# A two-block transformer kernel: first modulation columns on column quarters with zero products between, a third buffer for the modulation weights, and background steps tied to data

## The chip, the cores and the metric

The kernel runs on one core of a Trainium2 chip. TensorE (PE in the rows; PEld are its weight loads) does the matrix products, VectorE is DVE, ScalarE is ACT, GpSimd is POOL and SyncE is SP; POOL and SP here issue transfers almost alone. The metric is the device time of one launch in microseconds (us); less is better.

## The reference, cut to what matters

A first block of two layers (token mixer, then a gated convolutional feed-forward) runs on 256 latent and 256 context tokens of width 1024, then a second block (mLSTM and attention, then a product-key expert layer) on the result. Every normalised input is scaled and shifted by vectors that come from a conditioning vector alone:

```python
def adaln_params(cvec, w_ada, b_ada):
    m = jax.nn.silu(cvec) @ w_ada + b_ada        # 1024 -> 6144
    return jnp.split(m, 6, axis=-1)              # shift, scale, gate, shift, scale, gate
...
    h = modulate(rmsnorm(x, g1), sh1, sc1)       # the same with hc for the context
    z = h @ w_in
    ...
    x = x + gt1 * (mix @ w_out)
    x = x + gt2 * conv_ffn(modulate(rmsnorm(x, g2), sh2, sc2), w_up, ffn_conv, w_down)
```

There are three such weight matrices `w_ada` (two layers of the first block, one of the second), 25 MB each, used for one or two conditioning vectors (`c` for the latent tokens, `x` in the kernel's names for the context).

## The kernel before

All products run in fp32-like precision from two fp32r halves: `weight` loads a 128x1024 weight into `wraw` (three buffers, SP's queue), ACT rounds it to `whi` (L259), DVE makes the rest `wlo` (L262), and `gemm` does three products per tile (L278): hi·hi, hi·lo, lo·hi. A product with 512 columns is one matmul; 24 of them use up one weight of the first layer's feed-forward.

**The modulation vectors** are made in two ways. The first two sections of layer 0 (shift and scale of the first norm) are needed at once, and `first_norm` makes them on TensorE: four chunks of 512 outputs (`columns(0..3)`, scale and shift of the first 512 features, then of the last 512), whose weights `adan` (two transfers of 1 MB a chunk) are the moving operand while the silu of the two conditioning vectors (`cc_s`) is stationary, two columns wide. Chunks 0 and 1 are plain fp32 products (L421; each fp32 product is two matmuls in the trace), chunks 2 and 3 are split by ACT and DVE into `adah` and `adal` and done as fp32r products (L418, L419). ACT copies the sums to `adar` (L423), four small products (`po`, L426) turn the row into columns, DVE adds the bias (L432, L434). Meanwhile ACT squares `x` and `xc`, DVE adds them (`nacc`), TensorE sums over partitions (L479), DVE takes the inverse root from `nv` on (L481), and TensorE spreads it over partitions (`pt`, L494). Then `modulated` makes `nw` (L508, DVE), `h_hi` (L509, ACT) and `h_lo` (L510, DVE), and `tokens_gemm` multiplies them by `win_tm` (L666): 96 matmuls for `v` and `va`, then 96 for queries and keys (`pqk`), whose results pass DVE (`e`, L715) to transposes on TensorE (L721).

All other sections are made by `ada_chunk` in the background: POOL's queue loads 128 outputs x 1024 weights into `adaw` (512 KB, two buffers), and DVE multiplies by the silu vector `cvec` and sums along the row (`junk`, L365), one step for each conditioning vector. `background` gives these steps low priorities; the list scheduler places them in DVE's order between the layer's own work, once and for all at build time. Each engine then takes its instructions in that order. `later0` hands them out: 24 chunks of layer 0 in three lots (FIRST0 = 14, up to EARLY0 = 17, the rest), and in layer 0's feed-forward (`where == 3`) 66 two-vector or one-vector chunks of layers 0, 1 and 2, 122 DVE steps in all: 48 steps of two-vector chunks, 32 one-vector chunks of layer 1 (each with a transfer of its own), then 32 and 10 steps for the second block. Ahead of the last 42 come the second block's silu vectors (`load_cvec`): a transfer into an `adaw` buffer, a tanh on ACT (L354) into another, and a DVE step (L356).

The feed-forward (`ffn`) runs `up(0)`, `up(1)`, `down(0)`, `up(2)`, `down(1)`, `down(2)`: 68 weights in layer 0.

Of the kernel before, what the change touches and what calls it, by code (L numbers as in the profile page):

```python
# [11 lines left out]
F32 = mybir.dt.float32  # L12
F32R = mybir.dt.float32r
# [9 lines left out]
P = 128  # L23
D = 1024
# [11 lines left out]
RSQRT_MAGIC = 0x5F3759DF  # L36
NE = 128
# [38 lines left out]
def first_constants():  # L76
    k = Pack()
    k.add("ident", np.eye(P))
    k.add("ones", np.ones((P, P)))
    k.add("pairs", np.tile(np.eye(2), (2, 1)))  # L80
# [130 lines left out]
class Kernel:  # L211
# [137 lines left out]


    def load_cvec(self, idx, raw, th):

        self.nc.gpsimd.dma_start(raw, self.d["cvec"][idx].partition_broadcast(P))
        self.nc.scalar.activation(th, raw, AF.Tanh, scale=0.5)  # L354
# [29 lines left out]
    def first_norm(self, pool, tokens, hi, lo):  # L384
# [3 lines left out]
        cc = self.prm["ccol"]  # L388
        th = self.t(pool, [P, 2 * KT], F32, "cc_th", 1)
        nc.scalar.activation(th, cc, AF.Tanh, scale=0.5)  # L390
        s = self.t(pool, [P, KT, 2], F32, "cc_s", 1)
        nc.vector.scalar_tensor_tensor(s.rearrange("p a b -> p (a b)"), th, 1.0, cc, op0=OP.add, op1=OP.mult)
        s4 = self.t(pool, [P, KT, 4], F32R, "cc_s4", 1)
        self.split(s4[:, :, 0:2], s4[:, :, 2:4], s)
# [10 lines left out]
        def columns(ch):  # L405
            half, scale = ch // 2, ch % 2 == 0
            p = self.acc()
            n = 4 if half else 2
            for kp in range(KT // 2):
                raw = w[ch, kp // 2][:, kp % 2 * 2:kp % 2 * 2 + 2, :]  # L410
                if half:
                    wh = self.t(pool, [P, 2, 512], F32R, "adah", 2)
                    wl = self.t(pool, [P, 2, 512], F32R, "adal", 2)
                    self.split(wh, wl, raw)
                for kk in range(2):
                    kt = kp * 2 + kk
                    if half:
                        nc.tensor.matmul(p[0:4, :], s4[:, kt, :], wh[:, kk, :], start=kt == 0, stop=False)  # L418
                        nc.tensor.matmul(p[0:4, :], s4[:, kt, :], wl[:, kk, :], start=False, stop=kt == KT - 1)  # L419
                    else:  # L420
                        nc.tensor.matmul(p[0:2, :], s[:, kt, :], raw[:, kk, :], start=kt == 0, stop=kt == KT - 1)  # L421
            row = self.t(pool, [4, 512], F32, "adar", 2)
            nc.scalar.mul(row[0:n, :], p[0:n, :], 0.5)  # L423
            q = self.po()
            for j in range(4):
                nc.tensor.matmul(q[:, j * 2:j * 2 + 2], row[0:n, j * P:j * P + P], self.k["pairs"][0:n, :], start=True, stop=True)  # L426
# [10 lines left out]
        for kt in range(KT):  # L437
            self.squares(kt, ((self.x, TOK, None), (self.xc, TOK, None)))
# [11 lines left out]
        return ps  # L450

# [97 lines left out]
    def trunk_layer(self, l, cv, later):  # L549
# [9 lines left out]
        with ExitStack() as st:  # L559
# [45 lines left out]
            with ExitStack() as st2:  # L605
                fp = st2.enter_context(tc.tile_pool(name=f"ffn{l}", bufs=1, reuse_waits="tile"))
                first = None if full else self.first_up(l, fp)
                later(3)
# [75 lines left out]
    def mixer_d(self, l, mp, hi, lo, mix, lam, pva, fill, begin, later):  # L684
# [986 lines left out]
def build(ctx, tc, d, out, tap=None, stop=None):  # L1671
# [12 lines left out]
    def later0(where):  # L1684
        if where == 0:
            both.extend(zip(("l0c", "l0x"), k.vecs))
            third.extend([j for s in (2, 3, 4) for j in k.ada_jobs(ap, 0, s, both, "n2g0" if s == 4 else None)])
            k.background(third[:FIRST0], 55)
# [4 lines left out]
        if where == 3:  # L1693
            b1 = [("l1" + n[2], v) for n, v in both]
            jobs = k.ada_jobs(ap, 0, 5, both)
            jobs += [j for s in (1, 0) for j in k.ada_jobs(ap, 1, s, b1, "n1g1" if s == 1 else None)]
            jobs += [j for s in (2, 3, 4, 5) for j in k.ada_jobs(ap, 1, s, b1[:1], "n2g1" if s == 4 else None)]
            k.background(jobs, FSTEP)
            c2 = [k.load_cvec(j, *[k.t(ap, [P, D], F32, "adaw", 2) for _ in range(2)]) for j in (2, 3)]
            second.extend([("l2c", c2[0]), ("l2x", c2[1])])  # L1700
            more = [j for s in (1, 0) for j in k.ada_jobs(ap, 2, s, second, "nmix" if s == 1 else None)]
            rest.extend([j for s in (2, 3, 4, 5) for j in k.ada_jobs(ap, 2, s, second[:1], "nffn" if s == 4 else None)])
            k.background(more + rest[:EARLY2], FSTEP, FSTEP * len(jobs))
# [33 lines left out]
```

## Time and profile before

| | |
|---|---|
| median of 3 runs | 2045.8 us (2042.17 to 2057.86) |
| profiled execution | 2045.38 us, of which the span is 2043.6 us |
| busy share of the span | PE 97%, PEld 88%, DVE 82%, ACT 48%, POOL 3% |
| mean granted clock of TensorE | 0.989 of full speed |

A busy TensorE counts matmuls whose ends are modelled, so the number of matmuls in a stretch tells more than its busy share. Stretches that the text speaks of: the start (0 to 95 us), layer 0's feed-forward (about 270 to 640 us).

### The profile page before, as it was taken

Reading aid. Unit: us, or ns where it says so; the run is one execution under the profiler, and the core shown is the slowest. Engines: PE = TensorE matmul, PEld = TensorE weight load, DVE = VectorE, ACT = ScalarE, POOL = GpSimd, SP = SyncE. Lnnn points to the kernel's source line nnn. Section 1 sums busy time; section 2 is a strip of 40 time slices with the busy share of each in tenths; the row PEclk is TensorE's granted clock in tenths of the full one; section 3 lists DMA queues with packets and bytes.
Section 4 is the critical chain, followed back from the end, with each engine's and each line's share of the span. In section 5 each row is a group of like instructions: output and inputs, shape, how many; then the busy total and the mean of one; then the engine's idle time right before and its main releaser. Section 6 shows DMA issues by size and latency. Waiting matters only on the chain. (4 is left out here: it accounts for less than half of the span.)

```text
span 2043.6 us, 38424 instructions
## 1 busy us (share of the span) xinstructions
PE 1979.9 (97%) x15072; PEld 1804.8 (88%) x15072; DVE 1673.9 (82%) x3488; ACT 985.5 (48%) x1682; POOL 71.1 (3%) x138
## 2 busy tenths in 40 slices
PE   7999999998999999999999999999999999999999
PEld 3777778886888889999788888999999999999999
DVE  5898889876987689987767679988988898898775
ACT  5476343321324766545345654546544444444444
POOL 0100001111110000000000000000000000000000
PEclk9999999999999999999999999999999999999999
DMA  7631446776673346775243253454455555555554
GB/s 289 209 131 63 134 150 210 228 229 224 207 223 110 120 135 223 265 273 178 73 134 104 83 179 126 159 189 157 155 194 179 181 190 185 178 186 186 182 190 156
DMA packets 98965, 355.97 MB, mean 174 GB/s; under 512 B 11296, under 2 KB 12192, under 8 KB 97248
## 3 DMA queue, kind: packets, MB, share of 16 engines
q1 hardware_dynamic: 77616, 279.21, 41.3%
q0 software_dynamic: 19232, 70.72, 10.8%
q10 hardware_dynamic: 1936, 3.59, 0.5%
q8 instruction: 118, 1.93, 0.4%
q14 instruction: 63, 0.52, 0.1%
HBM read 352.42 MB, written 1.05 MB: 173 GB/s over the span
## 5 line engine op out<-in xcount | busy, mean ns | idle before, releaser
L259 ACT CAST whi<-wraw 128x1024 fp32r<-128x1024 f32 (+2 forms) x524 | 537.9, 1028 | 399.5 <-PE pH L278 100.2
L262 DVE TENSOR_TENSOR wlo<-wraw,whi 128x1024 fp32r<-128x1024 f32 (+3 forms) x552 | 628.2, 1141 | 102.4 <-ACT whi L259 100.7
L1549 PE MATMUL out<-w_hi,whi 128*128 128x256 f32 x1024 | 284.6, 278 | 0.2 <-ACT w_hi L268 0.2
L1549 PE MATMUL out<-w_hi,wlo 128*128 128x256 f32 x1024 | 283.1, 277 | 0.0
L1549 PE MATMUL out<-w_lo,whi 128*128 128x256 f32 x1024 | 282.8, 277 | 0.0
L365 DVE SCALAR_TENSOR_TENSOR junk<-adaw,cvec 128x1024 bf16<-128x1024 f32 x192 | 234.6, 1222 | 54.2 <-DMA adaw<-ada_in 52.6
L1549 PEld LDWEIGHTS out<-w_hi,whi 128*128 128x128 f32 x1024 | 192.4, 188 | 0.3 <-ACT w_hi L268 0.3
L1549 PEld LDWEIGHTS out<-w_hi,wlo 128*128 128x128 f32 x1024 | 192.4, 188 | 0.1
L1549 PEld LDWEIGHTS out<-w_lo,whi 128*128 128x128 f32 x1024 | 192.1, 188 | 0.1
L278 PE MATMUL acc<-h_hi,whi 128*128 128x256 f32 (+1 forms) x880 | 169.7, 330 | 11.0 <-DVE xc L642 4.9
L268 ACT CAST w_hi<-act 128x256 fp32r<-128x256 f32 x128 | 51.9, 406 | 236.7 <-PE out L1549 228.3
L278 PE MATMUL pH<-p_hi,whi 128*128 128x256 f32 x1128 | 160.5, 283 | 2.2 <-ACT act L1480 2.2
L278 PE MATMUL acc<-h_lo,whi 128*128 128x256 f32 (+1 forms) x880 | 161.0, 322 | 0.1
L278 PE MATMUL acc<-h_hi,wlo 128*128 128x256 f32 (+1 forms) x880 | 158.6, 320 | 0.5 <-DVE wlo L262 0.4
L278 PEld LDWEIGHTS acc<-h_hi,whi 128*128 128x128 f32 x880 | 131.9, 192 | 27.4 <-ACT h_hi L268 5.1
L278 PE MATMUL pH<-p_lo,whi 128*128 128x256 f32 x1128 | 153.9, 279 | 0.0
L278 PE MATMUL pH<-p_hi,wlo 128*128 128x256 f32 x1128 | 153.8, 279 | 0.0
L278 PEld LDWEIGHTS acc<-h_hi,wlo 128*128 128x128 f32 x880 | 131.2, 189 | 14.1 <-DVE wlo L262 1.2
L278 PEld LDWEIGHTS pH<-p_hi,whi 128*128 128x128 f32 x1128 | 141.1, 189 | 2.6 <-ACT act L1480 2.4
L278 PEld LDWEIGHTS acc<-h_lo,whi 128*128 128x128 f32 x880 | 131.8, 191 | 12.7 <-issue 0.3
L278 PEld LDWEIGHTS pH<-p_hi,wlo 128*128 128x128 f32 x1128 | 140.8, 189 | 0.0
L278 PEld LDWEIGHTS pH<-p_lo,whi 128*128 128x128 f32 x1128 | 140.6, 189 | 0.0
(572 smaller groups left out, 3293.2 us busy)
## 6 DMA issues: line engine op xcount, KB each, us to landing
adaw<-ada_in POOLq DMA_DIRECT2D x128, 512.0 KB, 4.5
wraw<-pu_in SPq DMA_DIRECT2D x128, 512.0 KB, 3.3
wraw<-pv_in SPq DMA_DIRECT2D x128, 512.0 KB, 3.4
wraw<-wup_in SPq DMA_DIRECT2D x88, 512.0 KB, 4.5
wraw<-win_fm_in SPq DMA_DIRECT2D x44, 512.0 KB, 3.7
wraw<-wdn_in SPq DMA_DIRECT2D x32, 512.0 KB, 4.5
wraw<-wout_in SPq DMA_DIRECT2D x24, 512.0 KB, 4.0
adan<-ada0n_in SPq DMA_DIRECT2D x8, 1024.0 KB, 15.0
```

Source lines behind the costliest of these rows:

```text
L259: nc.scalar.copy(hi[:, :n], raw[:, :n])
L262: nc.vector.tensor_sub(lo[:, s], raw[:, s], hi[:, s].bitcast(F32))
L268: self.nc.scalar.copy(hi, src)
L278: nc.tensor.matmul(ps, a[:, k, :], b[:, k, :], start=first and j == 0, stop=last and j == len(todo) - 1)
L365: nc.vector.scalar_tensor_tensor(junk, w, 0.5, cv, op0=OP.mult, op1=OP.mult, accum_out=self.ada[key][:, nt:nt + 1])
L1549: nc.tensor.matmul(part(m), x[:, m, :], y, start=False, stop=False)
```

## The change

Three things change in the code, and the scheduler's order with them. (1) `columns` treats all four chunks alike: plain fp32 products, the stationary operand widened from 2 to 32 columns by zeros, and the eight 128-row slices put on four 32-column quarters of the array in turn (`tile_position=(0, r)`), whose four partial sums the `pairs` products add. The splits `adah`/`adal` go. Between them `idle` puts products of a zero tile `z` (bf16, 128x512), 32 and 8 around the halves of chunk 0, one for each of the eight squares, and 4, 3, 3 after chunks 0 to 2; those after a chunk depend on its `adar` row through a DVE step that writes zeros made from it. (2) In layer 0's feed-forward the chunks use the pool `fp` with three `adaw` buffers in place of two, the second block's conditioning vectors are loaded ahead into `ap`'s two buffers, and the tanh goes into an `fp` buffer. (3) The constant 0.5 in the chunk step becomes a one-column tile `half`, made by `after` from a result that has to exist first: the last `v` copy for the first lot, and the last `h_lo` for the feed-forward's.

```diff
+    def after(self, x):
+        self.half = self.sm([P, 1], "half", bufs=1)
+        self.nc.vector.tensor_scalar(self.half.bitcast(I32), x.bitcast(I32), 0, HALF_BITS, op0=OP.bitwise_and, op1=OP.bitwise_or)
...
-        w = self.t(pool, [P, D], F32, "adaw", 2)
+        w = self.t(pool, [P, D], F32, "adaw", 2 if pool is self.ap else 3)
         nc.gpsimd.dma_start(w, self.d[f"ada{l}"][nt - 16 if l == 0 else nt])
         for key, cv in vecs:
-            junk = self.t(pool, [P, D], BF16, "junk", 1)
-            nc.vector.scalar_tensor_tensor(junk, w, 0.5, cv, op0=OP.mult, op1=OP.mult, accum_out=self.ada[key][:, nt:nt + 1])
+            junk = self.t(self.ap, [P, D], BF16, "junk", 1)
+            nc.vector.scalar_tensor_tensor(junk, w, self.half, cv, op0=OP.mult, op1=OP.mult, accum_out=self.ada[key][:, nt:nt + 1])
...
-            for kp in range(KT // 2):
-                raw = w[ch, kp // 2][:, kp % 2 * 2:kp % 2 * 2 + 2, :]
-                if half:
-                    wh = self.t(pool, [P, 2, 512], F32R, "adah", 2)
-                    wl = self.t(pool, [P, 2, 512], F32R, "adal", 2)
-                    self.split(wh, wl, raw)
...
-                        nc.tensor.matmul(p[0:2, :], s[:, kt, :], raw[:, kk, :], start=kt == 0, stop=kt == KT - 1)
-            row = self.t(pool, [4, 512], F32, "adar", 2)
-            nc.scalar.mul(row[0:n, :], p[0:n, :], 0.5)
+            for kt in range(KT):
+                r = kt % 4 * 32
+                if ch == 0 and kt % 4 == 0:
+                    self.idle(z, (32, 8)[kt // 4])
+                nc.tensor.matmul(p[r:r + 32, :], s[:, kt, :], w[ch, kt // 4][:, kt % 4, :], start=kt < 4, stop=kt >= 4, tile_position=(0, r))
+            row = self.t(pool, [P, 512], F32, "adar", 2)
+            nc.scalar.mul(row, p, 0.5)
+            if ch < 3:
+                self.idle(z, (4, 3, 3)[ch], row[:, 0:1])
...
         columns(0)
         for kt in range(KT):
+            self.idle(z, 1)
             self.squares(kt, ((self.x, TOK, None), (self.xc, TOK, None)))
...
+    def idle(self, z, n, x=None):
+        if x is not None:
+            self.nc.vector.tensor_scalar(z[:, 0:2].bitcast(I32), x.bitcast(I32), 0, 0, op0=OP.bitwise_and, op1=OP.bitwise_or)
+        p = self.att()
+        for _ in range(n):
+            self.nc.tensor.matmul(p, z[:, 0:P], z, start=True, stop=True)
...
+        if full:
+            self.after(v[:, 3, 0:1])
+            later("v")
...
         if where == 3:
+            k.after(k.h[1][:, KT - 1, 2 * TOK - 1:2 * TOK])
             b1 = [("l1" + n[2], v) for n, v in both]
-            jobs = k.ada_jobs(ap, 0, 5, both)
...
+            raws = []
+            for j in (2, 3):
+                raw = k.t(ap, [P, D], F32, "adaw", 2)
+                nc.gpsimd.dma_start(raw, k.d["cvec"][j].partition_broadcast(P))
+                raws.append(raw)
+            jobs = k.ada_jobs(fp, 0, 5, both)
...
-            c2 = [k.load_cvec(j, *[k.t(ap, [P, D], F32, "adaw", 2) for _ in range(2)]) for j in (2, 3)]
+            def vectors():
+                for j in (2, 3):
+                    second.append((("l2c", "l2x")[j - 2], k.silu2(j, raws[j - 2], k.t(fp, [P, D], F32, "adaw", 3))))
+            k.background([vectors], 0, FSTEP * len(jobs))
```

In TensorE's order at the start, the first `tokens_gemm` products (L666, in the changed file L680) stood ahead of most of chunk 2's products (L418, L419). Before:

```order
L494 MATMUL pt_208<-nacc_35_153,consts_73 128x128 x4
L421 MATMUL acc_217<-adan_109,cc_s_98 2x512
L421 MATMUL acc_217<-adan_111,cc_s_98 2x512 x4
L426 MATMUL po_228<-consts_73,adar_226 128x2 x4
L418 MATMUL acc_263<-adah_264,cc_s_17_100 4x512
L666 MATMUL att_359<-whi_114,h_hi_90 128x512
L666 MATMUL att_360<-whi_114,h_hi_90 128x512
L666 MATMUL att_361<-whi_114,h_hi_90 128x512
L666 MATMUL att_362<-whi_114,h_hi_90 128x512
```

After, at the same place (L423 are the quarter products, L430 the small ones that turn a row, L463 the zero products):

```order
L423 MATMUL acc_332<-adan_125,cc_s_100 32x512 x4
L423 MATMUL acc_332<-adan_127,cc_s_100 32x512 x4
L430 MATMUL po_348<-consts_73,adar_341 128x2 x4
L463 LDWEIGHTS idle_96
L463 MATMUL att_344<-idle_96 128x512
...
L680 MATMUL att_385<-whi_114,h_hi_90 128x512 x2
L680 MATMUL att_385<-whi_114,h_lo_91 128x512
L423 MATMUL acc_357<-adan_129,cc_s_100 32x512 x4
L680 MATMUL att_385<-whi_114,h_lo_91 128x512
```

The first token product now stands behind the whole of chunk 2, with its row and three zero products. A little ahead of this, twelve zero products stand between the fifth and the sixth of the eight products that sum the squares (L492):

```order
L430 MATMUL po_192<-consts_73,adar_184 128x2 x4
L492 MATMUL acc_247<-consts_73,nacc_39_203 128x1
...
L463 LDWEIGHTS idle_96
L463 MATMUL att_187<-idle_96 128x512
...
L463 MATMUL att_242<-idle_96 128x512
L492 MATMUL acc_247<-consts_73,nw_244 128x1
```

Before, the eight stood together, ahead of chunk 0's small products.

ACT's order after, at the start: chunk 2's row `adar_341` stands behind all eight `h_hi` of the first half, of which these are the last.

```order
L522 ACTIVATE h_hi_90<-nw_318,ada_l0x_78 128x256
L522 ACTIVATE h_hi_90<-nw_325,ada_l0c_77 128x256
L522 ACTIVATE h_hi_90<-nw_325,ada_l0x_78 128x256
L425 ACTIVATE adar_341<-acc_332 128x512
L363 ACTIVATE adan_375<-adan_375 128x1024
```

So the first token product waits for DVE's work on the whole first half, through this row.

DVE's order in the feed-forward, the last one-vector chunks. Before, two chunk steps (L365) stand to a weight (L262):

```order
L262 TENSOR_TENSOR wlo_4292<-wraw_4290,whi_4291 128x1024
L365 SCALAR_TENSOR_TENSOR junk_2750,ada_l1c_79<-adaw_2748,cvec_78_352 128x1024
L365 SCALAR_TENSOR_TENSOR junk_2754,ada_l1c_79<-adaw_2752,cvec_78_352 128x1024
L642 SCALAR_TENSOR_TENSOR x_67<-acc_4223,ada_l0c_77,x_67 128x256
L642 SCALAR_TENSOR_TENSOR xc_89<-acc_4223,ada_l0x_78,xc_89 128x256
L262 TENSOR_TENSOR wlo_4325<-wraw_4323,whi_4324 128x1024
```

After (L374 is the chunk step, L263 the weight's, L365 the silu step of the second block's vectors, whose transfers now stand some fifty chunks earlier on POOL's queue):

```order
L263 TENSOR_TENSOR wlo_4322<-wraw_4320,whi_4321 128x1024
L374 SCALAR_TENSOR_TENSOR junk_2800,ada_l1c_79<-adaw_2798,half_2520,cvec_75_378 128x1024
L374 SCALAR_TENSOR_TENSOR junk_2804,ada_l1c_79<-adaw_2802,half_2520,cvec_75_378 128x1024
L656 SCALAR_TENSOR_TENSOR x_67<-acc_4253,ada_l0c_77,x_67 128x256
L656 SCALAR_TENSOR_TENSOR xc_89<-acc_4253,ada_l0x_78,xc_89 128x256
L263 TENSOR_TENSOR wlo_4355<-wraw_4353,whi_4354 128x1024
L374 SCALAR_TENSOR_TENSOR junk_2808,ada_l1c_79<-adaw_2806,half_2520,cvec_75_378 128x1024
L365 SCALAR_TENSOR_TENSOR cvec_711_2817<-adaw_2815,adaw_2524 128x1024
L365 SCALAR_TENSOR_TENSOR cvec_709_2813<-adaw_2811,adaw_2522 128x1024
```

The two silu steps stand together now and wait for no transfer issued just before. Over all, the 32 one-vector chunks are spread over 16 weights before and over 13 after. On POOL's and DVE's queues no chunk stands behind another wait than that for its own buffer, before and after.

## Rows read from the trace of the kernel before

**Rows 1.** Busy time by stretch: matmuls in brackets, then PEclk, DMA share, GB/s.

```profile
33.00:38.00 5.00, 4.53 (x13) 2.99 (x13) 5.00 (x11) 4.99 (x10) 0.00 (x0) 0.66 1.02 406
...
470.00:480.00 10.00, 9.56 (x42) 7.55 (x41) 6.85 (x11) 2.11 (x2) 1.11 (x3) 1.00 0.78 240
480.00:490.00 10.00, 6.29 (x27) 4.56 (x26) 7.03 (x12) 0.00 (x0) 2.11 (x4) 1.00 0.75 254
490.00:500.00 10.00, 8.34 (x36) 6.50 (x35) 4.97 (x8) 1.99 (x2) 0.53 (x1) 1.00 0.53 149
500.00:510.00 10.00, 7.88 (x28) 6.00 (x27) 4.52 (x7) 3.52 (x4) 1.05 (x2) 0.83 0.65 211
510.00:520.00 10.00, 10.00 (x45) 8.11 (x44) 9.93 (x15) 4.68 (x6) 1.05 (x2) 1.00 0.57 185
```

**Rows 2.** Timeline, 490 to 502 us: start, length, engine; in brackets the idle time before.

```profile
494.85 1.06 ACT L354 ACTIVATE adaw<-adaw 128x1024 f32<-128x1024 f32 x1 [17.68 <-DMA adaw<-cvec_in]
...
497.46 0.53 POOL L353 DMA_DIRECT2D adaw<-cvec_in  x1 [8.13 <-DVE cvec L356]
```

**Rows 3.** DVE's waits from 420 to 560 us: total, times, longest.

```profile
DVE junk L365 <- DMA adaw<-ada_in: 24.1, 20, 2.9
```

**Rows 4.** Timeline of the start.

```profile
17.69 0.40 ACT L463 ACTIVATE nw<-xc 128x256 f32<-128x256 f32 x1
...
19.58 0.38 PE L479 MATMUL acc<-consts,nacc 128*128 128x1 f32 x2
19.68 0.59 ACT L423 ACTIVATE adar<-acc 2x512 f32<-2x512 f32 x1 [1.59 <-PE acc L421]
...
21.56 0.16 DVE L481 TENSOR_SCALAR nv<-acc 128x4 f32<-128x4 f32 x1 [2.63 <-PE acc L479]
...
25.51 1.16 PE L494 MATMUL pt<-nacc,consts 128*128 128x128 f32 x8
...
26.60 4.45 PE L421 MATMUL acc<-adan,cc_s 128*2 128x512 f32 x10
...
26.71 0.48 DVE L508 SCALAR_TENSOR_TENSOR nw<-x,ada_l0c,pt 128x256 f32<-128x256 f32 x1 [0.96 <-PE pt L494]
27.11 0.47 DVE L508 SCALAR_TENSOR_TENSOR nw<-xc,ada_l0x,pt 128x256 f32<-128x256 f32 x1
...
28.28 1.22 DVE L262 TENSOR_TENSOR wlo<-wraw,whi 128x1024 fp32r<-128x1024 f32 x1
...
31.73 1.05 PE L426 MATMUL po<-consts,adar 2*128 2x2 f32 x8 [0.68 <-ACT adar L423]
...
33.02 0.51 ACT L509 ACTIVATE h_hi<-nw,ada_l0c 128x256 fp32r<-128x256 f32 x1 [0.40 <-DVE ada_l0c L432]
...
33.58 1.25 PE L666 MATMUL att<-whi,h_hi 128*128 128x512 f32 x4 [0.47 <-ACT h_hi L509]
```

**Rows 5.** TensorE's timeline where queries and keys end.

```profile
84.42 0.63 PE L666 MATMUL acc<-whi,h_lo 128*128 128x512 f32 x2
...
89.04 0.62 PE L666 MATMUL po<-wlo,h_hi 128*128 128x512 f32 x2
92.47 1.82 PE L721 MATMUL att<-consts,e 128*128 128x128 f32 x8 [2.82 <-DVE e L715]
93.94 3.06 PE L278 MATMUL acc<-h_hi,whi 128*128 128x512 f32 x8
```

**Rows 6.** The same timeline where attention's value products stand on two column halves.

```profile
122.14 1.09 PE L799 MATMUL po<-aT,vtm 128*64 128x128 f32 x14
```

**Rows 7.** DVE groups by shape: busy us, mean ns; L780 reads a one-column scalar.

```profile
L269 DVE TENSOR_TENSOR g_lo<-f_s,g_hi 128x512 fp32r<-128x512 f32 x22 | 15.1, 686 | 0.0
...
L780 DVE SCALAR_TENSOR_TENSOR e<-e,rsm,e 128x512 f32<-128x512 f32 x16 | 12.0, 747 | 2.1 <-ACT e L779 2.1
```

**Rows 8.** Transfers of 420 to 500 us (KB, median us to landing); then all of `adaw`.

```profile
adaw<-ada_in POOLq DMA_DIRECT2D x21, 512.0 KB, 4.6
...
DMA to landing us min/median/max: 3.6/4.5/7.9
```

More of the change, by code (lines that the diff above doesn't have):

```diff
@@ L36 @@
 RSQRT_MAGIC = 0x5F3759DF
+HALF_BITS = 0x3F000000
 NE = 128
@@ L388, in first_norm @@
         cc = self.prm["ccol"]
+        z = self.t(pool, [P, 512], BF16, "idle", 1)
+        nc.vector.memset(z, 0.0)
         th = self.t(pool, [P, 2 * KT], F32, "cc_th", 1)
         nc.scalar.activation(th, cc, AF.Tanh, scale=0.5)
[L391 to L394, printed above, removed]
+        s = self.t(pool, [P, KT, 32], F32, "cc_s", 1)
+        nc.gpsimd.memset(s, 0.0)
+        nc.vector.scalar_tensor_tensor(s[:, :, 0:2], th.rearrange("p (a b) -> p a b", b=2), 1.0, cc.rearrange("p (a b) -> p a b", b=2), op0=OP.add, op1=OP.mult)
         w = {}
@@ L407, in columns @@
             p = self.acc()
-            n = 4 if half else 2
-            for kp in range(KT // 2):
-                raw = w[ch, kp // 2][:, kp % 2 * 2:kp % 2 * 2 + 2, :]
-                if half:
-                    wh = self.t(pool, [P, 2, 512], F32R, "adah", 2)
-                    wl = self.t(pool, [P, 2, 512], F32R, "adal", 2)
-                    self.split(wh, wl, raw)
[L415 to L420, printed above, removed]
-                        nc.tensor.matmul(p[0:2, :], s[:, kt, :], raw[:, kk, :], start=kt == 0, stop=kt == KT - 1)
-            row = self.t(pool, [4, 512], F32, "adar", 2)
-            nc.scalar.mul(row[0:n, :], p[0:n, :], 0.5)
+            for kt in range(KT):
[7 more added lines that the diff above has]
+                self.idle(z, (4, 3, 3)[ch], row[:, 0:1])
             q = self.po()
             for j in range(4):
-                nc.tensor.matmul(q[:, j * 2:j * 2 + 2], row[0:n, j * P:j * P + P], self.k["pairs"][0:n, :], start=True, stop=True)
+                nc.tensor.matmul(q[:, j * 2:j * 2 + 2], row[:, j * P:j * P + P], self.k["pairs"], start=True, stop=True)
             qv = q[:, 0:8].rearrange("p (j v) -> p v j", v=2)
@@ L1687, in later0 @@
             third.extend([j for s in (2, 3, 4) for j in k.ada_jobs(ap, 0, s, both, "n2g0" if s == 4 else None)])
+        if where == "v":
             k.background(third[:FIRST0], 55)
@@ L1693, in later0 @@
         if where == 3:
+            k.after(k.h[1][:, KT - 1, 2 * TOK - 1:2 * TOK])
             b1 = [("l1" + n[2], v) for n, v in both]
-            jobs = k.ada_jobs(ap, 0, 5, both)
-            jobs += [j for s in (1, 0) for j in k.ada_jobs(ap, 1, s, b1, "n1g1" if s == 1 else None)]
-            jobs += [j for s in (2, 3, 4, 5) for j in k.ada_jobs(ap, 1, s, b1[:1], "n2g1" if s == 4 else None)]
-            k.background(jobs, FSTEP)
-            c2 = [k.load_cvec(j, *[k.t(ap, [P, D], F32, "adaw", 2) for _ in range(2)]) for j in (2, 3)]
-            second.extend([("l2c", c2[0]), ("l2x", c2[1])])
-            more = [j for s in (1, 0) for j in k.ada_jobs(ap, 2, s, second, "nmix" if s == 1 else None)]
+            fp = k.fp
+            raws = []
[4 more added lines that the diff above has]
+            jobs = k.ada_jobs(fp, 0, 5, both)
+            jobs += [j for s in (1, 0) for j in k.ada_jobs(fp, 1, s, b1, "n1g1" if s == 1 else None)]
+            jobs += [j for s in (2, 3, 4, 5) for j in k.ada_jobs(fp, 1, s, b1[:1], "n2g1" if s == 4 else None)]
+            k.background(jobs, FSTEP)
+            def vectors():
+                for j in (2, 3):
+                    second.append((("l2c", "l2x")[j - 2], k.silu2(j, raws[j - 2], k.t(fp, [P, D], F32, "adaw", 3))))
+            k.background([vectors], 0, FSTEP * len(jobs))
+            more = [j for s in (1, 0) for j in k.ada_jobs(fp, 2, s, second, "nmix" if s == 1 else None)]
+            early = [j for s in (2, 3) for j in k.ada_jobs(fp, 2, s, second[:1])]
             rest.extend([j for s in (2, 3, 4, 5) for j in k.ada_jobs(ap, 2, s, second[:1], "nffn" if s == 4 else None)])
-            k.background(more + rest[:EARLY2], FSTEP, FSTEP * len(jobs))
+            k.background(more + early[:EARLY2], FSTEP, FSTEP * len(jobs))
     k.trunk_layer(0, None, later0)
```

5 lines of the change are left out of this document (4 added, 1 removed).

## The prediction

> **What bounds the kernel now.** TensorE is busy for 97% of the span, so only stretches in which it does fewer matmuls than its full rate can give anything back. I read first the busy time by stretch, counting matmuls; then, where they are missing, the timeline and the waits of the engine that TensorE waited for; then the order before and after at those places. The change touches two: the start (to about 95 us) and layer 0's feed-forward.
>
> In the feed-forward 10 us hold 45 products of 512 columns at full rate, .222 us each. From 470 to 510 us they hold 42, 27, 36 and 28: 133 in place of 180 [rows 1]. The missing 47 are 10.4 us, and no other stretch of the feed-forward lacks as many. The cause is on ACT: its tanh (L354) stood idle 17.68 us for the second block's conditioning vector [rows 2], with every later rounding of a weight behind it in ACT's order; the second vector's transfer waited 8.13 us on POOL for a buffer. Both queue behind the chunk steps, which are late themselves: DVE waited 24.1 us for their weights between 420 and 560 us [rows 3]. The arithmetic fits. A buffer's turn is landing 4.6 [rows 8], issue .53 [rows 2] and the DVE step, 1.22 by a step of the same size [rows 4]: 6.35, with two buffers 3.18 us per one-vector chunk. A weight lasts TensorE 24 x .222 = 5.33 us, and 32 such chunks lie over 16 weights, 2.67 us each. Each chunk is .51 late, the 32 together 16 us, more than the two weights that three buffers hold ahead (10.7 us).
>
> At the start TensorE makes its first token product at 33.58 and ends queries and keys at 89.04 + .46 = 89.5 [rows 4, 5], with chunk 2's and 3's columns between. At 33 to 38 us the granted clock is .66 (partly at 1.2, partly at 2.4 GHz) after a stretch with little but a row of small products [rows 1, 4]. After 89.5 it waits 2.82 us for DVE's `e`, behind chunk steps, and the next eight products take 3.06 us [rows 5].
>
> **The change part by part: the feed-forward.** The conditioning vectors are loaded before its first chunks are used up, so the tanh waits for no transfer of its own. If nothing else is late there, all 10.4 us come back; this cannot be more, since TensorE is otherwise at rate. What is late next? The chunk steps. The scalar `half` is read from memory, and a DVE step with such a scalar takes .747 us against .686 without [rows 7], .061 more; 122 steps in the feed-forward make 7.4 us of DVE time, covered by the 24.1 us of waits that three buffers take away. A turn is now 4.6 + .53 + 1.28 = 6.41, over three buffers 2.14 us. But the scheduler has spread the 32 one-vector chunks over 13 weights, not 16: 13 x 5.33 / 32 = 2.17 us each. So the third buffer is used up almost to the last by the denser order: it is just in time, without reserve except the two weights held ahead. I take back 1.0 us of the 10.4 (between 0 and the 32 x .061 = 2.0 that the scalar costs where it is tight): **-9.4 us**.
>
> **The start.** Chunk 0's row needs ACT, whose last square ends at 18.1; with the copy .59 and the small products 1.05 [rows 4] that is 19.7. The sums of squares took from 19.58 to `nv` at 21.56, 2.0 us, and now come after, with twelve zero products in their midst. No row has a zero product; as one matmul of 512 columns it is bounded by .231 us (twenty token products from 84.42 to 89.04 [rows 5]) and twice that at 1.2 GHz: 2.8 to 5.5 us. `nv` comes at 24.5 to 27.2, not 21.56. From `nv` to the first `nw` are 5.15 us [rows 4]: 29.7 to 32.4. DVE then has eight `nw` and five `h_lo`, .40 us apart (26.71 to 27.11), and two weight steps of 1.22, 7.6 us, before the eighth `h_hi`; with that (.51), chunk 2's row behind it on ACT (.59), its small products (1.05) and three zero products (.7 to 1.4) the first token product stands at 40.2 to 43.6 us, seven to ten later than before.
>
> In return the path from there is shorter. Before, it took 55.9 us. Now it has 192 products of .231 (44.4), chunk 3 and one set of small products (1.05). A chunk without quarters costs sixteen matmuls of .43 (ten from 26.60 in 4.45 us [rows 4]), 6.9 us. Two column halves already work side by side here: fourteen matmuls of 128 columns in 1.09 us, .078 each, against 1.16 / 8 = .145 for L494's of the same length on the whole array [rows 4, 6]. I take a quarter, 1.7 us, with 3.4 and 6.9 as ends. That gives 47.2 us, up to 2.0 more if the clock is at .66 again for 5 us: the end of queries and keys at 87.4 to 92.8, in the middle .6 later than the 89.5 of before. The removed ACT and DVE splits (eight each) were beside TensorE's work and give nothing of their own.
>
> The Trainium skill ("TensorE: Matmul & The Clock Gate", Part 3) reports 2.38 times for three column tiles, less than one for one. By that figure chunk 3 would cost about 2.9 us, and the end would come 1.2 later; the two halves in this trace show nearly a full factor of two, and no row has three or four.
>
> Behind it the wait for `e` can go (2.82 us) and with it the slow products (eight at .231 are 1.85, not 3.06): 4.0 us. The first chunk step now waits for the last `v` copy, half of the 192 products on, at about 66 to 70 us, two transfers having landed before; of 28 steps eleven, not thirteen, stand ahead of `e`. The two left over, 2.6 us, and the scalar's .061 on all 28 (1.7 us) are done later, in a stretch in which DVE is nearly as full as TensorE. I keep -1.6 of the -4.0. Together the start gives **-1.0 us**, between -6.1 and +3.3.
>
> The steps that the second `half` holds back were not ahead of the last `h_lo` before either, so that part is costed at nothing; its cover is the order itself. Later layers only get the scalar: 22 steps x .061, 1.3 us of DVE time beside TensorE's work.
>
> **Sum.** -9.4 - 1.0 = -10.4 us. Against the profiled execution, 2045.38 us of which 1.8 lie around the span, that is 2035.0; the median of the runs shown is .4 higher. **Predicted: 2035 us**, .5% less.
>
> **The rivals.** *The good ends meet.* The zero products run and keep the clock at 2.4 GHz, the end of queries and keys is 87.4, the whole 4.0 us behind it come back, and the feed-forward gives all 10.4: -6.1 - 10.4 = -16.5, 2029 us. Against it speaks that between the halves of chunk 0 and the sums there is little for TensorE but small products, after which the clock fell at 33 us. Some of what DVE postpones would also have to vanish for more than 1%.
>
> *The quarters do not work side by side*, so the change does not do what it says. Chunk 0's second half would pass ACT's squares by 1.4 us, chunk 1's by 2.6, chunk 3 costs 5.2 more: 9.2, and 2044 us. The halves speak against it [rows 6], though they are not quarters.
>
> *The third buffer is outrun, and the kernel is slower.* Place: the 13 weights with the 32 one-vector chunks, 45 transfers of .524 MB in 69 us, 340 GB/s, where before 48 took 85 us. At 470 to 490 us a DMA share of .78 and .75 goes with 240 and 254 GB/s [rows 1], which puts the limit at 308 to 339: the demand stands at it. DVE's order is fixed, so a late chunk holds back the `wlo` behind it and so TensorE. If landing goes to the longest seen, 7.9 us [rows 8], a chunk takes 3.24 us, 1.07 late, the 32 together 34; less the 10.7 held ahead 23.5 us of stall, which eats the 10.4 and leaves +12: 2057 us. The kernel is slower than before from a landing of about 6.8 us on. Against it: at 308 GB/s the 45 transfers take 76.6 us, 7.3 too many, still within the 10.7.
>
> The Trainium skill ("Trainium Kernel Development and Optimization", Key Constraints) says that transfers from SP, ACT and POOL run on the same 16 engines and interleave. By that rule the third buffer buys nothing beyond the engines' limit and this rival's mechanism holds; the landing of 4.6 at a share of .75 to .78 does not yet show it.
>
> **How the numbers follow.** The forecast's own case, 2031 to 2040, has a chance of .55. The good ends (2024 to 2031) have .17, of which .09 are below 2025, the quarters without effect or a start at its bad end (2040 to 2048) .16, the outrun buffer (over 2048) .12, of which .05 are above 2066. The range 2024 to 2048 leaves out about .15. The runs of before lie .8% apart, so 1% (20 us) is about what a measurement can tell from no change: faster by over 1% .09, slower by over 1% .05, within 1% .86.
>
> **What would show it.** In the profile after: no long wait of ACT at the tanh, about 45 matmuls in every 10 us of the feed-forward, DVE's waits for `adaw` in it well below 24 us, a landing below 6 us; the first token product near 42 us, queries and keys ending near 90, and a short wait for `e` or none. I am wrong if the first token product comes by 36 us, if TensorE lacks products where the one-vector chunks are, or if the stretch from 95 to 270 us changes by more than 5 us, for which I have no term.

## The result, and the profile after

The changed kernel is slower: median 2073.22 us (four runs, 2072.33 to 2076.91) against 2050.36 us of the kernel before (four runs, 2042.17 to 2057.86). The ratio is 1.0114 (95% interval 1.0087 to 1.0140). The forecast was 2035 us with a range up to 2048: wrong in sign and outside its range. The profiled execution took 2076.91 us.

The page says that TensorE is as busy as before, in a longer span (busy us, share, instructions):

```profile
span 2075.1 us, 38525 instructions
...
PE 2017.1 (97%) x15130; PEld 1840.2 (89%) x15130; DVE 1678.8 (81%) x3485; ACT 978.3 (47%) x1673; POOL 71.4 (3%) x139
```

So I looked for the 31.5 us where they were forecast first. Busy time by stretch in layer 0's feed-forward, the answer to [rows 1], and after it the waits there, the answer to [rows 2, 3]:

```profile
470.00:480.00 10.00, 10.00 (x45) 8.04 (x44) 9.38 (x15) 4.12 (x4) 1.58 (x3) 1.00 0.69 225
480.00:490.00 10.00, 10.00 (x45) 8.04 (x44) 8.85 (x14) 2.10 (x2) 1.05 (x2) 1.00 0.73 258
490.00:500.00 10.00, 10.00 (x45) 8.12 (x44) 9.89 (x17) 2.34 (x3) 1.11 (x3) 1.00 0.74 247
500.00:510.00 10.00, 10.00 (x45) 8.15 (x44) 9.96 (x15) 3.24 (x5) 1.32 (x3) 1.00 0.60 215
```

```profile
DVE junk L374 <- DMA adaw<-ada_in: 8.2, 11, 2.5
...
ACT adaw L363 <- DMA adaw<-ada_in: 3.8, 1, 3.8
```

All 180 products are there, the tanh waits 3.8 us and not 17.68, DVE 8.2 us for chunks and not 24.1. This part did what was forecast. The start, the answer to [rows 4, 5]:

```profile
22.12 4.99 PE L463 MATMUL att<-idle 128*128 128x512 bf16 x12
...
27.71 0.16 DVE L494 TENSOR_SCALAR nv<-acc 128x4 f32<-128x4 f32 x1 [7.12 <-PE acc L492]
...
31.62 0.48 DVE L521 SCALAR_TENSOR_TENSOR nw<-x,ada_l0c,pt 128x256 f32<-128x256 f32 x1 [0.67 <-PE pt L507]
...
34.93 1.92 PE L423 MATMUL acc<-adan,cc_s 128*32 128x512 f32 x16
...
43.76 1.42 PE L680 MATMUL att<-whi,h_hi 128*128 128x512 f32 x2
...
92.70 0.62 PE L680 MATMUL po<-wlo,h_hi 128*128 128x512 f32 x2
93.16 1.03 PE L738 MATMUL att<-consts,e 128*128 128x128 f32 x8
93.95 2.11 PE L279 MATMUL acc<-h_hi,whi 128*128 128x512 f32 x8
...
97.77 1.09 PE L738 MATMUL att<-consts,e 128*128 128x128 f32 x8 [1.02 <-DVE e L732]
```

The twelve zero products cost 4.99 us and the first token product comes at 43.76, but the eight products L279 start at 93.95, as they did at 93.94. Up to there the start has cost nothing; the stretch behind it is taken up further down.

The loss is at the end, in a stage whose code the change does not touch: the experts (L1549 before, L1566 after). First and last start of one of its three product groups, before and then after:

```profile
L1549 PE MATMUL out<-w_hi,whi x1024: 275/277/383, 1448.2 to 2038.7; 128*128 128x256 f32 x171
```

```profile
L1566 PE MATMUL out<-w_hi,whi x1024: 277/281/385, 1455.6 to 2070.3; 128*128 128x256 f32 x171
```

That is 590.5 us before and 614.7 after: 24.2 of the 31.5 us. TensorE hardly waits there (nothing before, 0.2 us once after). Busy time by stretch from 1500 to 1900 us (TensorE alone; before, then after) shows the same 400.00 us busy at the same clock, with 161 products fewer:

```profile
1500.00:1900.00 400.00, 400.00 (x3962) 1.00 0.56 184
```

```profile
1500.00:1900.00 400.00, 400.00 (x3801) 1.00 0.52 176
```

On the timeline each product of 256 columns simply comes later after the one before it. Eight of them take 0.90 or 0.91 us from start to start before, 0.94 or 0.95 after: 113 and 118 ns (starts of groups in sequence; the lengths hold a modelled end):

```profile
1608.92 1.07 PE L278 MATMUL pH<-p_hi,whi 128*128 128x256 f32 x8
1609.83 1.07 PE L278 MATMUL pH<-p_lo,whi 128*128 128x256 f32 x8
1610.73 1.07 PE L278 MATMUL pH<-p_hi,wlo 128*128 128x256 f32 x8
```

```profile
1622.75 1.11 PE L279 MATMUL pH<-p_hi,whi 128*128 128x256 f32 x8
1623.69 1.11 PE L279 MATMUL pH<-p_lo,whi 128*128 128x256 f32 x8
1624.64 1.11 PE L279 MATMUL pH<-p_hi,wlo 128*128 128x256 f32 x8
```

What did the change do to these products? Their instructions are the same, in the same order. But the new tile `half`, 4 bytes a partition in the pool `small`, takes a place of 32 bytes in the compiled program, and every tile placed behind it stands 32 bytes further: `p_hi` at 72,992 in place of 72,960, `w_hi` at 224,544 in place of 224,512. The weights `whi` and `wlo` lie ahead of it and stay (`whi` at 42,560). The rest of the work was to find out whether that is the cause, and by what rule.

### The profile page after: what moved, and what is told of

Same layout as the page of the kernel before. It is cut to its first block, busy times and chain, and to the rows that moved or that the text cites. A ratio compares the mean times of both kernels' runs of the same rounds, so it can differ in the third digit from the quotient of the medians.

```text
span 2075.1 us, 38525 instructions
## 1 busy us (share of the span) xinstructions
PE 2017.1 (97%) x15130; PEld 1840.2 (89%) x15130; DVE 1678.8 (81%) x3485; ACT 978.3 (47%) x1673; POOL 71.4 (3%) x139
## 3 DMA queue, kind: packets, MB, share of 16 engines
HBM read 352.42 MB, written 1.05 MB: 170 GB/s over the span
## 4 chain that ended last, share of the span: by engine, by line
PE 80%; DVE 10%; DMA 4%; issue 3%; ACT 3%; POOL 0%; SPq 0%; DVEq 0%; ACTq 0%; POOLq 0%
PE acc L279 21%; PE out L1566 18%; PE pH L279 17%; PE att L279 10%; PE att L680 3%; DVE wlo L263 2%; DMA adaw<-ada_in 2%; PE pg L1535 1%; ACT whi L260 1%; PE acc L680 1%; PE po L680 1%; PE pt L680 1%; DVE junk L374 1%; PE pg L1529 1%; DVE ri L1582 1%
## 5 line engine op out<-in xcount | busy, mean ns | idle before, releaser
L263 DVE TENSOR_TENSOR wlo<-wraw,whi 128x1024 fp32r<-128x1024 f32 (+3 forms) x552 | 626.6, 1138 | 120.3 <-ACT whi L260 115.6
L1566 PE MATMUL out<-w_hi,whi 128*128 128x256 f32 x1024 | 289.0, 282 | 0.2 <-ACT w_hi L269 0.2
L1566 PE MATMUL out<-w_hi,wlo 128*128 128x256 f32 x1024 | 287.6, 281 | 0.0
L1566 PE MATMUL out<-w_lo,whi 128*128 128x256 f32 x1024 | 287.1, 281 | 0.0
L374 DVE SCALAR_TENSOR_TENSOR junk<-adaw,half,cvec 128x1024 bf16<-128x1024 f32 x192 | 245.8, 1280 | 22.3 <-DMA adaw<-ada_in 20.5
L1566 PEld LDWEIGHTS out<-w_hi,whi 128*128 128x128 f32 x1024 | 193.0, 188 | 0.3 <-ACT w_hi L269 0.3
L1566 PEld LDWEIGHTS out<-w_hi,wlo 128*128 128x128 f32 x1024 | 193.0, 189 | 0.1
L1566 PEld LDWEIGHTS out<-w_lo,whi 128*128 128x128 f32 x1024 | 192.8, 188 | 0.0
L279 PE MATMUL acc<-h_hi,whi 128*128 128x256 f32 (+1 forms) x880 | 171.1, 331 | 7.3 <-ACT h_hi L269 2.2
L279 PE MATMUL pH<-p_hi,whi 128*128 128x256 f32 x1128 | 164.2, 286 | 1.9 <-ACT act L1497 1.9
L279 PE MATMUL acc<-h_lo,whi 128*128 128x256 f32 (+1 forms) x880 | 163.3, 324 | 0.0
L279 PE MATMUL acc<-h_hi,wlo 128*128 128x256 f32 (+1 forms) x880 | 159.2, 321 | 0.5 <-DVE wlo L263 0.5
L279 PE MATMUL pH<-p_hi,wlo 128*128 128x256 f32 x1128 | 157.8, 282 | 0.0
L279 PE MATMUL pH<-p_lo,whi 128*128 128x256 f32 x1128 | 157.8, 282 | 0.0
L279 PEld LDWEIGHTS acc<-h_hi,whi 128*128 128x128 f32 x880 | 133.9, 194 | 22.9 <-ACT h_hi L269 4.7
L279 PEld LDWEIGHTS pH<-p_hi,whi 128*128 128x128 f32 x1128 | 144.4, 189 | 2.2 <-ACT act L1497 2.1
L279 PEld LDWEIGHTS acc<-h_hi,wlo 128*128 128x128 f32 x880 | 132.4, 191 | 13.8 <-DVE wlo L263 0.7
L279 PEld LDWEIGHTS pH<-p_hi,wlo 128*128 128x128 f32 x1128 | 144.5, 189 | 0.0
L279 PEld LDWEIGHTS pH<-p_lo,whi 128*128 128x128 f32 x1128 | 144.2, 189 | 0.0
L279 PEld LDWEIGHTS acc<-h_lo,whi 128*128 128x128 f32 x880 | 133.1, 193 | 12.2 <-DVE wlo L263 0.2
```

Source lines behind the costliest of these rows:

```text
L263: nc.vector.tensor_sub(lo[:, s], raw[:, s], hi[:, s].bitcast(F32))
L279: nc.tensor.matmul(ps, a[:, k, :], b[:, k, :], start=first and j == 0, stop=last and j == len(todo) - 1)
L374: nc.vector.scalar_tensor_tensor(junk, w, self.half, cv, op0=OP.mult, op1=OP.mult, accum_out=self.ada[key][:, nt:nt + 1])
L1566: nc.tensor.matmul(part(m), x[:, m, :], y, start=False, stop=False)
```

## The experiments

In all kernels but the bench, the products looked at here have `whi` or `wlo` as stationary operand and `p`, `w` or `g` (hi and lo) as moving operand. The number that sorts the runs turned out to be the distance from `whi` to the moving tile, modulo 256 bytes: before, 72,960 - 42,560 = 118 x 256 + 192 for `p`, and also 192 for `w`. The table has it, the products of 1500 to 1900 us from the same row as above, and the ratio of the times.

| kernel | distance of p, w | products | ratio (95%) |
|---|---|---|---|
| before | 192, 192 | 3962 | |
| after | 224, 224 | 3801 | 1.0114 (1.0087 to 1.0140) |
| e1_half64 | 0, 0 | 3759 | 1.0145 (1.0119 to 1.0170) |
| e2_before_pad32 | 224, 224 | 3801 | 1.0159 (1.0136 to 1.0181) |
| e3_p_only | 224, 0 | 3781 | 1.0165 (1.0140 to 1.0191) |
| e4_stationary | 224, 224 | 3812 | 1.0164 (1.0132 to 1.0196) |
| e5_all32 | 192, 192 | 3961 | 1.0011 (0.9997 to 1.0025) |
| e6_half128 | 64, 64 | 3824 | 1.0102 (1.0083 to 1.0121) |
| e7_ffn128 | 64, 64 | 3824 | 1.0107 (1.0085 to 1.0129) |
| e8_start | 192, 192 | 3961 | 1.0004 (0.9989 to 1.0018) |
| e9_half_const | 192, 192 | 3961 | 0.9965 (0.9950 to 0.9981) |
| e10_ffn_const | 192, 192 | 3960 | 0.9975 (0.9960 to 0.9991) |
| e11_ffn1_place | 192, 192 | 3961 | 0.9964 (0.9949 to 0.9979) |

**First four: is it the place?** The first theory was that products come at their full rate only if the moving tile begins on a multiple of 64 bytes.

```diff
-        self.half = self.sm([P, 1], "half", bufs=1)
+        self.half = self.sm([P, 16], "half", bufs=1)[:, 0:1]
```

> The changed kernel, but the small tile `half` is 64 bytes a partition in place of 4, so that all tiles placed behind it stand 64 bytes further than in the kernel before and not 32. Theory (place): the expert stage's 256-column products start 118.3 ns apart in the changed kernel and 113.3 before because their moving operands (p_hi, p_lo, w_hi, w_lo) now begin 32 bytes off a multiple of 64; here they go back to 113 ns, the stage gets back its 25 us, and the time is 2073 - 25 - 3 (the same in the feed-forwards' second halves) = 2042 to 2050 us. Rival (the change's own instructions or their order slow the later stages, or the pointer scalar does): the size of an unused part of a tile changes nothing, 118 ns and 2073 us.

```diff
+        if full:
+            self.sm([P, 1], "pad", bufs=1)
         part = {} if full else {2: (256, 512), 3: (256, 512)}
```

> The kernel before, with one unused tile of 4 bytes in the small pool at the place where the change puts `half`; no instruction is added. Theory (place): every tile behind it stands 32 bytes further, the expert stage's products go from 113 to 118 ns apart, and the kernel loses 25 to 30 us (ratio 1.012 to 1.015). Rival (the slowdown belongs to the change's instructions): ratio 1.000.

```diff
+            self.t(pp, [P, 8], F32, "pad0", 1)
             hi = self.t(pp, [P, KT, TOK], F32R, "p_hi")
...
             ep = st.enter_context(tc.tile_pool(name="experts", bufs=1, reuse_waits="tile"))
+            self.t(ep, [P, 8], F32, "pad1", 1)
```

> The kernel before, with an unused 32-byte tile ahead of p_hi and p_lo (the moving operand of the experts' first products) and another ahead of w_hi (the moving operand of the second), so that p_hi and p_lo stand 32 bytes off and w_hi and w_lo again on a multiple of 64. Theory (place of the moving operand): the products pH<-p_hi, p_lo go to 118 ns, out<-w_hi, w_lo stay at 113 ns, and the kernel loses half of 25 us, 11 to 14 us (ratio 1.006). Rival (some other tile's place decides, the gates G or the transfers' landing places): both groups slow, or neither.

```diff
         self.small = pool("small", 3)
+        self.t(self.wp, [P, 8], F32, "pad0", 1)
+        self.t(self.small, [P, 8], F32, "pad1", 1)
```

> The kernel before, with an unused 32-byte tile ahead of the weight buffers wraw, whi and wlo, and another behind them, so that the weights (stationary operand of the feed-forward's and the experts' products) stand 32 bytes off and all other tiles again on the multiple of 64 that they had. Theory (moving operand only): the experts' products stay at 113 ns; only the token products, where the weights are the moving operand (L666, 560 of 512 columns), lose some 5 ns each, 3 us in all: ratio 1.000 to 1.002. Rival (either operand's place counts): 118 ns, and 25 us or more.

All four are slow. e2 settles half of the question: the kernel before, with not one instruction more, loses 1.6% through an unused tile of 4 bytes, and its products count 3801, exactly those of the changed kernel. It is the place. But the theory of the multiple of 64 fell: with 64 bytes (e1) there are fewer products still (3759), and with `w` back on a multiple of 64 (e3) or all moving tiles on one (e4) it is as bad. e4 shows more: moving tiles 64 further and weights 32 further give within 0.3% the count of moving tiles 32 further alone. So the distance between the two operands could be what counts.

**The distance.**

```diff
         self.small = pool("small", 3)
+        self.t(self.wp, [P, 8], F32, "pad0", 1)
```

> The kernel before, with one unused 32-byte tile ahead of the weight buffers, so that the weights and everything behind them stand 32 bytes further: no tile of the feed-forwards or the expert stage begins on its old multiple of 64, but the distance from whi and wlo to p_hi, p_lo, w_hi, w_lo and g is what it was. Theory (the distance between the two operands counts, modulo 128 bytes; in the last four runs every place with a moved distance was slow, and a shift of both by 32 gave the cadence of a shift of one by 32): 113.3 ns in the expert stage, 229 ns in the first feed-forward's second half, ratio 0.999 to 1.002. Rival (each tile's own multiple of 128 counts): 118 to 120 ns and ratio 1.015.

The theory holds, on this row and in the time (1.0011): no tile of these products stands where it stood, their distances are the old ones, and the products are back.

```profile
1500.00:1900.00 400.00, 400.00 (x3961) 1.00 0.54 184
```

**The period, and the change's parts.** e6 and e7 put 128 bytes for `half` (e7 with the first norm of before), e8 is the kernel before with the change's first part alone.

```diff
+        self.half = self.sm([P, 32], "half", bufs=1)[:, 0:1]
```

> The changed kernel with 128 bytes for `half` in place of 4: every tile behind it stands 128 bytes further than in the kernel before. Theory (distance modulo 128): 113.3 ns in the expert stage, the 25 us and some 3 us of the feed-forwards come back, and what is left is the change's own: 10 us won in the first feed-forward, some 4 lost at the start: ratio 0.994 to 0.999. Rival (any move from the places of before is slow, or the period is longer than 128): 118 to 120 ns and ratio 1.011 to 1.016.

> As e6_half128, but with the first norm of the kernel before (columns, splits and pairs as they were, no zero products): the change's second and third part alone. Theory: the first feed-forward's 10 us without the start's loss: ratio 0.993 to 0.997, 2 to 5 us below e6_half128. Rival (my prediction's sum: the start gains 1 us): e6_half128 is the faster by 1 us.

> The kernel before with the change's first part alone (column quarters, zero products, pairs); no tile behind the first norm is moved. Theory: the first token product comes at 41 to 44 us against 33.6, queries and keys end 2 to 4 us later, ratio 1.001 to 1.002; expert stage 113.3 ns. Rival (my prediction's sum): ratio 0.9995.

A period of 128 is refuted: e6 and e7 have 3824 products and are 1% slow. The feed-forward's gain can't be read from them, then. At the same distances they still compare the start: e6, which has it, is 2.0 us faster by the medians (2070.24 against 2072.28), where its theory had it 2 to 5 us slower; the two intervals overlap. In e8 the start alone is 1.0004, within 0.2% of nothing, and the theory and its rival can't be told apart.

**The law.** The bench does nothing of the reference's work (the input is copied to the output).

```diff
+    def products(name, n, step, off):
+        p = pp.tile([P, 512], F32, tag="ps", name=name, bufs=2)
+        for t in range(3):
+            for k in range(KT):
+                a = off + k * step
+                nc.tensor.matmul(p[:, :n], st[:, k, :], mv[:, a:a + n], start=t == 0 and k == 0, stop=t == 2 and k == KT - 1)
...
+    for j in range(32):
+        products(f"rows{32 * j:04d}b", 256, 256, 8 * j)
```

> Nothing of the reference's work but products that are not used: 32 groups of 24 fp32r products each for three shapes (256 columns with the moving rows 1,024 bytes apart, as p_hi; 512 columns, rows 2,048 bytes apart, as g; 256 columns with one moving row for all, as w_hi), the stationary tile fixed and the moving tile's first byte 0, 32, ... 992 bytes further than 4,096 behind it; the input is copied to the output. Theory (distance between the operands): the cadence changes from group to group in a pattern that repeats within 512 bytes or less (a stationary row is 512 bytes), between 113 and 120 ns for 256 columns and by 4 to 5 ns for 512. Rival (the products' cadence depends on what VectorE, ScalarE and the transfers do beside them): one cadence for all 32 groups of a shape, since nothing runs beside them here.

One period of the first shape (the first groups differ: see the last section), and three groups of the second, with 512 columns (timeline; the name has the bytes of offset; 24 products a group, so the difference of two starts, by 24, is the spacing):

```profile
56.45 3.04 PE L1690 MATMUL rows0256b<-mv,st 128*128 128x256 f32 x24
59.32 3.00 PE L1690 MATMUL rows0288b<-mv,st 128*128 128x256 f32 x24
62.16 2.99 PE L1690 MATMUL rows0320b<-mv,st 128*128 128x256 f32 x24
64.99 3.03 PE L1690 MATMUL rows0352b<-mv,st 128*128 128x256 f32 x24
67.85 3.01 PE L1690 MATMUL rows0384b<-mv,st 128*128 128x256 f32 x24
70.70 2.98 PE L1690 MATMUL rows0416b<-mv,st 128*128 128x256 f32 x24
73.52 2.89 PE L1690 MATMUL rows0448b<-mv,st 128*128 128x256 f32 x24
76.25 3.00 PE L1690 MATMUL rows0480b<-mv,st 128*128 128x256 f32 x24
79.08 3.04 PE L1690 MATMUL rows0512b<-mv,st 128*128 128x256 f32 x24
...
180.04 5.67 PE L1690 MATMUL wide0320b<-mv,st 128*128 128x512 f32 x24
185.54 5.77 PE L1690 MATMUL wide0352b<-mv,st 128*128 128x512 f32 x24
191.16 5.76 PE L1690 MATMUL wide0384b<-mv,st 128*128 128x512 f32 x24
```

With 256 columns the eight places of a period (offset 0, 32, ... 224 modulo 256) are 119.6, 118, 118, 119, 119, 117.5, **113.8** and 118 ns apart: one place in eight is fast in this period, 192, which is where `p` and `w` of the kernel before lie. 224 is the changed kernel's, 64 that of e6 and 0 that of e1; the counts of the table agree, 3962 at 192, some 3800 at 224 and 64, and the least at 0. e3 has two places in one kernel: in its expert loop the products of `p` (224) come 0.95 us a row of eight, some 118 ns apart, and those of `w` (0) 2.64 us for 22, which is 120 ns. With 512 columns 64 (g's distance before; offset 320) gives 5.50 / 24 = 229 ns, and 96 (after) 5.62 / 24 = 234. The third shape, one moving row for all, repeats the first. Nothing ran beside, so VectorE, ScalarE and transfers have no part in it.

**A place for `half` that moves no distance.** The const pool lies ahead of the weights. e10 has, besides, the first norm of before.

```diff
-        self.half = self.sm([P, 1], "half", bufs=1)
+        self.half = self.t(self.cp, [P, 1], F32, "half", 1)
```

> The changed kernel with `half` in the const pool, which lies ahead of the weight buffers: the weights and all that lies behind them move by 32 bytes together, so that each distance is that of the kernel before (g in the first feed-forward is 12,288 bytes further, three buffers of 4,096). Theory (distance between the two operands of a product): 113.3 ns in the expert stage, 229 ns for the products of g, and the time is that of the change's own steps: 10 us won in the first feed-forward, 0 to 4 lost at the start: ratio 0.995 to 0.999, 2040 to 2048 us. Rival (the change slows the late stages in another way as well): 117 ns or more and ratio over 1.005.

> As e9_half_const, with the first norm of the kernel before: the feed-forward's three buffers and the held steps alone, at the distances of the kernel before. Theory: the 10 us of the first feed-forward without the start, which alone measured 1.0004 (0.9989 to 1.0018): ratio 0.994 to 0.997, as e9_half_const within 3 us. Rival (the start costs the 4 us that its profile shows): 4 us below e9_half_const.

Both are faster than the kernel before, with intervals clear of 1, as their theories said. e9's median is 2042.55 us (2039.64 to 2045.42) against 2050.03. The changed kernel, with the same steps and `half` at the other place, had 2073.22: by the medians the place alone costs some 31 us, about as much as in e2 (1.0159, that is 32.6). e10's rival, that the start costs 4 us, is refuted: without the start's change the median is 2044.32, 1.8 us above e9 and not 4 below. Group g in layer 0's feed-forward, first and last start: before, after, e9.

```profile
L278 PE MATMUL att<-g_hi,whi x94: 279/392/395, 440.6 to 638.9; 128*128 128x512 f32 x82, 128*128 128x256 f32 x12
```

```profile
L279 PE MATMUL att<-g_hi,whi x94: 278/394/400, 445.1 to 634.9; 128*128 128x512 f32 x82, 128*128 128x256 f32 x12
```

```profile
L279 PE MATMUL att<-g_hi,whi x94: 279/392/394, 441.7 to 629.2; 128*128 128x512 f32 x82, 128*128 128x256 f32 x12
```

That is 198.3, 189.8 and 187.5 us: the stage is 10.8 us shorter at the old distance and 8.5 at the new one.

**One more tile placed.** The law says that layer 1's g (distance 64, 256 columns) would gain at 192.

```diff
+        if l:
+            self.t(fp, [P, 32], F32, "pad", 1)
+
         def up(gi):
```

> As e9_half_const, with an unused tile of 128 bytes ahead of g in the second layer's feed-forward, which moves g_hi and g_lo from distance 64 to distance 192 (modulo 256) behind the weights; nothing else of the computation moves by it but that stage's own small tiles. Theory (the law of bench_distance: 118.0 ns at 64, 113.7 at 192 for 256 columns): the 528 products of g there, 117.8 ns apart in the kernel before, come 113.7 apart, 2.2 us in all, if the stage is bound by them: ratio 0.994 to 0.998. Rival (that stage waits for its weights' transfers anyway): 113.7 ns too, but the 2.2 us go into waits of the products for wlo and whi, and the stage is as long as in e9_half_const. Second rival (the law is that of the bench alone): 118 ns.

Half right. In the kernel before, the products of all three groups take 0.94 us a row of eight (118 ns). In e11 those of the last two take 0.905 (113 ns), as in this piece of its timeline. But the products of the first group (866 to 887 us) stayed at 118, so the gain is some 1.5 us, which the time cannot show: 0.9964, as e9. In e6 and e7 the 128 bytes of `half` had put this g at 192 already, and there the products of all three groups come 113 ns apart.

```profile
930.33 1.07 PE L279 MATMUL att<-g_lo,whi 128*128 128x256 f32 x8
931.24 1.07 PE L279 MATMUL att<-g_hi,wlo 128*128 128x256 f32 x8
932.14 1.07 PE L279 MATMUL acc<-g_hi,whi 128*128 128x256 f32 x8
```

## Why the prediction was wrong

**The step that failed** is "Later layers only get the scalar: 22 steps x .061". I costed the scalar's instruction and put its tile at nothing. The 32 bytes moved the distance between stationary and moving operand in the expert stage from 192 to 224: 24.2 us of the 31.5 between the two spans, and some 31 us by the medians of e9 and the changed kernel, all stages together. I had compared instructions and their order where the change touches them, and elsewhere took equal instructions for equal durations. No rival covered it; the one that ended slower, the outrun third buffer, did not happen (28 chunks of 420 to 500 us landed in 4.9 us at the median, against 21 in 4.6 [rows 8]). The limit of 308 to 339 GB/s that this rival worked out was too low as well: a line of [rows 1] itself has 406 GB/s, at a share of 1.02.

**The feed-forward, -9.4 us**: right. The cause was the one named, the 47 missing products came back, and the stage is 10.8 us shorter where g keeps its distance (e9), just above the 10.4 at which I had capped it. The 1.0 that I took off for a tight third buffer was not lost. At the moved distance 2.3 us of it went, by the same failed step. The scalar costs what was forecast: the chunk step takes 1280 ns on the mean in place of 1222, 58 ns against the 61 read from other steps, and its waits cover it.

**The start, -1.0 us**: not refuted in its size, but its terms were off both ways. `nv` came at 27.71 (forecast up to 27.2). The twelve zero products took 4.99 us, inside their bounds, but the granted clock was at .50 to .53 from 17 to 27 us, mostly the level of 1.2 GHz, where it was at 1.00 before; so the small products and the sums ahead of them, which I had priced by rows of before, were slow too (eight small products 1.87 us in place of 1.05). The first token product came at 43.76 (up to 43.6), the end of queries and keys at 92.70 + .46 = 93.2 (up to 92.8). What stands against it was right: no wait for `e` is left ahead of the first eight L279 products, which take 2.11 us in place of 3.06 (one wait of 1.02 us stands behind them), so that all is level at 94 us (e2 and e5, with the start of before, begin these products at 95.4 and 98.1).

From there to the second norm the changed kernel loses 5.2 us, where I had 2.4 for the postponed work of DVE (the 4.0 less the 1.6 that I kept). A change by more than 5 us between 95 and 270 us was the prediction's own sign of being wrong. TensorE's timeline before, then after, and a wait after that before does not have:

```profile
262.78 0.79 PE L494 MATMUL po<-nacc,consts 128*128 128x128 f32 x4 [1.55 <-DVE nacc L493]
```

```profile
267.94 0.71 PE L507 MATMUL po<-nacc,consts 128*128 128x128 f32 x4 [1.54 <-DVE nacc L506]
```

```profile
PE acc L926 <- ACT dft_g L927: 2.5, 1, 2.5
```

It repeats: from the first eight products at about 94 us to this row it is 168.8 to 170.1 us in the kernel before, e2 and e5, 173.0 to 174.0 in the five kernels with all parts of the change, 175.7 in e8, which has the first part alone, and 177.4 and 177.9 in e7 and e10, which lack it. So the first part and the held chunk steps of the third each go with a longer stretch, and what delays it stays open. In the whole time the start alone is 1.0004 (e8), that is -2 to +4 us, and beside the other parts it is some 2 us faster in both pairs (e6 and e7, e9 and e10), hardly clear of the noise.

**The quarters** work side by side. Sixteen products of a chunk take 1.92 us, where sixteen at .43 were 6.9: 3.6 times (forecast 1.7 us, four times). The rival without that effect is refuted. By the figure of 2.38 for three tiles that I cited from the Trainium skill ("TensorE: Matmul & The Clock Gate", Part 3) an estimate for the chunk is 2.9 us. Its table has no row for four column tiles, and the 1.92 us here decide.

**Between 640 and 1448 us** the lead shrank in each profile: from 4.0 ahead to 7.4 behind in the changed kernel, from 9.7 ahead to 0.8 ahead in e9. But e5, with the instructions of before, fell back 3 us there too: the profiled execution of before was a quick one (2045.38, with medians of 2049 to 2052). What the other 6 us in e9 are stays open: e10, with e9's steps there, fell back 3.6 (4.5 ahead to 0.9). In layer 1's feed-forward DVE waited 8.9 us for chunks in the changed kernel and 3.7 before, but 4.4 in e9, so this is not it there. Overall e9 wins 7.2 us by its ratio (4 to 10), not the 10.4 of the forecast.

## What to carry to other kernels

A new tile, however small, moves the tiles placed behind it (4 bytes took 32 here), and a kernel that is bound by TensorE can lose more by that than the change can win: before a changed kernel is judged, compare where the operands of its busiest products lie, and put new small tiles where they move no distance. When a stage whose code did not change takes longer with TensorE busy throughout, count its products per stretch: the busy share hides, and the modelled durations (277 and 281 ns) hardly show, what the count (3962 and 3801) shows.

## What was not expected of the hardware

In the bench, where nothing else differs or runs, products of two fp32r operands with 256 columns start 113 to 120 ns apart by the distance between stationary and moving tile, with a period of 256 bytes; with 512 columns, 228 to 234 ns. A shift of both operands together changes nothing (e5).

The distance does not settle it alone. In the bench the first four groups (offsets 0 to 96) are in another phase: there 64 is the fast one (its 24 products go from 39.62 to 42.34, 113 ns); from 192 on that place is the fast one and 64 is not. In the kernel before, ahead of the expert loop, stretches of products at distance 192 run at 113 or at 118 ns, and change from one to the other only where other products come between, as here at one transposition:

```profile
1362.82 1.07 PE L278 MATMUL pH<-p_lo,whi 128*128 128x256 f32 x8
1363.73 1.08 PE L278 MATMUL pH<-p_hi,wlo 128*128 128x256 f32 x8
1364.64 0.27 PE L1661 MATMUL pg<-consts,pf 128*128 128x128 f32 x1
1364.67 1.19 PE L278 MATMUL pH<-p_hi,whi 128*128 128x256 f32 x8
1365.69 1.10 PE L278 MATMUL pH<-p_lo,whi 128*128 128x256 f32 x8
1366.64 0.64 PE L278 MATMUL pH<-p_hi,wlo 128*128 128x256 f32 x4
```

At 192 all rows of the expert loop are in the fast phase; at 224 and 0 no row of it or ahead of it is. What sets the phase, and why e11's first group is in the slow one, was not tried.
